# One step of a two-layer diffusion backbone: a new order of weights and of sums over k, and attention scores in double PSUM banks

## The chip, the core and the metric

The kernel runs on one core of a Trainium2 chip, with the engines TensorE (PE in the profile; its weight loads PEld), VectorE (DVE), ScalarE (ACT), GpSimd (POOL) and SyncE (SP, which issues the large loads). The metric is the device time of one execution in microseconds (us), the median of several; lower is better.

## What is computed

One step of a two-layer diffusion backbone on 640 tokens: 128 context tokens and 512 latent tokens, width 1024, all in fp32. The first 128 columns of every tile are context, the rest latent. Cut to what matters:

```python
for i in range(2):
    mod = (silu(cond) @ ada_w[i] + ada_b[i])        # 9 vectors of 1024, for c and for c_ctx
    h = rms_norm(x) * (1 + mod[1]) + mod[0]
    x = x + 0.5 * mod[2] * swiglu(h)                # ffn (i,0): 1024 -> 2 x 2816 -> 1024
    h = rms_norm(x) * (1 + mod[4]) + mod[3]
    x = x + mod[5] * (even_mixer(h) if i == 0 else odd_mixer(h))
    h = rms_norm(x) * (1 + mod[7]) + mod[6]
    x = x + 0.5 * mod[8] * swiglu(h)                # ffn (i,1)
# even mixer: 4 retention heads, and 4 groups of u * (w_s @ rms_norm(gelu(v)) + b_s)  ("SGU")
# odd mixer: 8 heads of differential attention over 640 keys:
s = einsum(q, k) * scale                            # two maps j = 0, 1 for each head
p = softmax(s);  a = p[0] - lam * p[1];  o = rms_norm(a @ v)
```

## The kernel before

**Products.** Activations lie with the features on the partitions and the 640 tokens in two halves of 320 columns. Every weight tile of 1 MB comes from HBM into one of two `raw` buffers, and is split in pieces of 128x1024 into a high part (`whi`, a copy on ACT, L308) and a low part (`wlo`, a subtraction on DVE, L309); five pieces may be live. Each product is then three matmuls (L695 high x high, L696 low x high, L697 high x low) of 128x320, accumulated in one PSUM bank.

**Stages.** ffn(0,0), even mixer, ffn(0,1), ffn(1,0), odd mixer, ffn(1,1). An ffn has 22 groups of 256 hidden features in chunks of 6, 8 and 8: for each group an input product ("fin", the last 19 groups by Strassen's scheme, evacuated to activations `a<l><s><g>h` and `...l`), and at the end of a chunk four output groups ("fout"), which sum over the chunk's groups. `out_proj` (L812) goes through the four, `op_step` (L837) through two column tiles j and two token halves hf of each: one PSUM tile `op...` for each (j, hf), all k of the chunk in a row, then the update of `xs` on DVE (L807).

**The order of weights.** One list, `order`, fixes it; SP loads a tile of it when a `raw` buffer is free (`pump`). Into the list `weave` (L223) puts the tiles of `ada_w` from which `mod` is made: one (`ads`) behind each entry that isn't a fin, and one (`pads`) ahead of each fin whose number stands in `FA`. A tile named in `ADV` is worked off on DVE (`ada_v`, L391: four passes over 128x1024, L404 for layer 0 and L406 for layer 1), others on PE (`ada`, L431: 32-column matmuls, L447, and at the fourth tile of a vector a copy to SBUF and two transposes). Each holds a `raw` buffer until it is done. In layer 1 vectors 0 to 5 are DVE's, 6 to 8 PE's.

**The engines' order.** Code is written in one thread with generators in the background (`spawn`, `tick`): each product of PE lets the background take a step. A scheduler sets the order on PE, DVE and ACT from that and from priorities (`high_priority(HP)`); SP's is the order in which it is written.

**Even mixer.** `sgu` (L1180) waits until its normalized `vs[g]` is ready, lets `SGW` = 11 steps pass and issues the mixing product `mx` (L1186). `load_condb` (L186) loads the conditioning, a tile of 128x2048, and runs Silu over it on ACT; it is called at the end of `first_wide`, the first product of ffn(0,0).

**Odd mixer.** A unit is one head and 128 queries: 8 heads of 4 full units (640 keys) and one of the context (128 keys). `sm_a` (L1292) takes for a full unit four PSUM tiles `as` of one bank of the eight (two maps j by two halves of the keys), runs 8 matmuls, four maxima on DVE (L1316), two minima (L1319) that join the halves, four exponentials on ACT with their sums (L1324); `sm_b` (L1328) joins the sums, and normalizes. Transposes, the product with the values and an rms norm of the head follow in the background, and the output groups ("oout", PSUM tiles `oo`) are woven between.

**Prologue.** `first_wide` and the code from L1500 on make the first two vectors of `mod` from PE, normalize x and begin ffn(0,0); two pieces there and two in `first_wide` are split with GpSimd as the subtracting engine (`split_piece(nc.gpsimd)`).

## Time and profile before

| | us |
|---|---|
| median of 3 runs | 2477.71 (2469.72 to 2481.81) |
| profiled execution, its time | 2478.16 |
| profiled execution, its span | 2476.1 |
| TensorE busy / weight load busy | 2395.3 (97%) / 2342.1 (95%) |
| VectorE busy | 1840.8 (74%) |
| ScalarE busy | 1067.4 (43%) |
| GpSimd busy | 63.7 (3%) |
| mean granted clock of TensorE | 0.987 |

The span runs from the first to the last instruction of the profiled execution; the time has some 2 us around it. A matmul's shown duration runs past the start of the next one, since they are pipelined; what a stretch of matmuls costs is read from their starts, and what a wait costs from the idle time ahead of the instruction that waited.

### The profile page before, as it was taken

The numbers are of one execution on the slowest core, as the hardware profiler recorded it, in microseconds if no ns is written. First come the engines' busy times: TensorE is split into PE (matmuls) and PEld (weight loads), VectorE is DVE, ScalarE is ACT, GpSimd is POOL, SyncE is SP. The second block draws the span as 40 slices with busy tenths as digits, with TensorE's granted clock in tenths as the row PEclk, the third lists the DMA queues.
The fourth block names the chain that finished last, engine by engine and source line by source line (L and its number), as shares of the span: only waits on it lengthen the run. The fifth ranks groups of instructions, "written<-read, shape, count | busy, mean of one in ns | idle before, by whom it ended". The sixth has DMA issues, their size and how long they took to land.

```text
span 2476.1 us, 40714 instructions
## 1 busy us (share of the span) xinstructions
PE 2395.3 (97%) x16530; PEld 2342.1 (95%) x16530; DVE 1840.8 (74%) x3749; ACT 1067.4 (43%) x2018; POOL 63.7 (3%) x86
## 2 busy tenths in 40 slices
PE   8999999999899999999999999999999999999998
PEld 6899999899899999999999999999999989999998
DVE  7677867877878777677977776789788878574664
ACT  4525335333226335153542423536777646252442
POOL 1000000000000000000000000001011000000000
PEclk8999999999999999999999999999999999999999
DMA  7342423323231433423234242242111111222121
GB/s 277 112 151 86 154 71 115 137 105 124 79 136 69 137 120 119 153 96 124 91 108 145 96 175 89 103 171 74 42 43 57 54 35 67 81 87 91 69 103 43
DMA packets 44476, 259.30 MB, mean 105 GB/s; under 512 B 5889, under 2 KB 8577, under 8 KB 16769
## 3 DMA queue, kind: packets, MB, share of 16 engines
q1 hardware_dynamic: 41024, 252.37, 28.6%
q8 instruction: 129, 2.11, 0.4%
q0 software_dynamic: 1280, 2.62, 0.3%
q10 hardware_dynamic: 1984, 1.72, 0.2%
q14 instruction: 59, 0.48, 0.1%
HBM read 252.76 MB, written 3.93 MB: 104 GB/s over the span
## 4 chain that ended last, share of the span: by engine, by line
PE 80%; DVE 9%; DMA 4%; ACT 4%; issue 2%; POOL 0%; POOLq 0%; ACTq 0%; DVEq 0%
PE op L696 8%; PE op L697 8%; PE op L695 8%; PE pu L695 6%; PE pu L696 6%; PE pu L697 6%; PE pg L697 3%; DVE wlo L309 3%; PE pg L696 3%; PE pg L695 3%; PE pf L695 3%; PE pf L696 3%; PE pf L697 3%; ACT whi L308 2%; DMA raw<-in_w_fout 2%
## 5 line engine op out<-in xcount | busy, mean ns | idle before, releaser
L309 DVE TENSOR_TENSOR wlo<-raw,whi 128x1024 fp32r<-128x1024 f32 (+1 forms) x480 | 528.8, 1118 | 286.0 <-ACT whi L308 284.9
L308 ACT ACTIVATE whi<-raw 128x1024 fp32r<-128x1024 f32 (+1 forms) x484 | 465.0, 976 | 639.7 <-DMA raw<-in_w_fout 144.1
L807 DVE SCALAR_TENSOR_TENSOR xs<-op,mod,xs 128x128 f32<-128x128 f32 (+2 forms) x312 | 126.9, 435 | 135.1 <-PE op L697 134.6
L524 ACT ACTIVATE nq<-xs 128x320 f32<-128x320 f32 x84 | 39.0, 468 | 135.1 <-DVE xs L807 133.3
L406 DVE CUSTOM_DVE_ANT_0 raw<-raw,sb 128x1024 f32<-128x1024 f32 x72 | 87.4, 1218 | 0.7
L404 DVE SCALAR_TENSOR_TENSOR raw<-raw,sb 128x1024 f32<-128x1024 f32 x72 | 87.5, 1220 | 0.5
L695 PE MATMUL oq<-H4h,whi 128*128 128x320 f32 x256 | 81.1, 318 | 0.2 <-ACT ov L979 0.2
L697 PE MATMUL oq<-H4h,wlo 128*128 128x320 f32 x256 | 79.6, 311 | 0.0
L696 PE MATMUL oq<-H4l,whi 128*128 128x320 f32 x256 | 79.3, 310 | 0.0
L1316 DVE TENSOR_REDUCE amx<-as 128x1 f32<-128x320 f32 x144 | 61.5, 460 | 19.1 <-PE as L1312 18.8
L1324 ACT ACTIVATE ap<-as,anm 128x320 f32<-128x320 f32 x128 | 66.2, 531 | 14.1 <-DVE anm L1319 13.9
L696 PE MATMUL pf<-H5p,whi 128*128 128x320 f32 x172 | 53.8, 313 | 2.0 <-DVE H5p L614 2.0
L871 ACT COPY p<-pg 128x320 f32<-128x320 f32 x76 | 32.5, 427 | 53.8 <-PE pg L697 53.6
L696 PE MATMUL pf<-H3p,whi 128*128 128x320 f32 x172 | 53.5, 312 | 1.8 <-DVE H3p L614 1.8
L696 PE MATMUL pf<-H2p,whi 128*128 128x320 f32 x172 | 53.4, 312 | 1.8 <-DVE H2p L614 1.8
L695 PE MATMUL pf<-H0p,whi 128*128 128x320 f32 x172 | 54.3, 318 | 0.2 <-ACT H0p L609 0.2
L696 PE MATMUL pf<-H0p,whi 128*128 128x320 f32 x172 | 53.9, 313 | 0.2 <-DVE H0p L614 0.2
L695 PE MATMUL pf<-H5p,whi 128*128 128x320 f32 x172 | 53.9, 317 | 0.0
L695 PE MATMUL pf<-H3p,whi 128*128 128x320 f32 x172 | 53.8, 317 | 0.0
L695 PE MATMUL pf<-H2p,whi 128*128 128x320 f32 x172 | 53.8, 316 | 0.0
L291 DVE TENSOR_TENSOR raw<-raw 128x512 f32<-128x512 f32 x76 | 52.4, 689 | 1.9
L697 PE MATMUL pf<-H0p,wlo 128*128 128x320 f32 x172 | 53.8, 313 | 0.0
(2691 smaller groups left out, 8835.6 us busy)
## 6 DMA issues: line engine op xcount, KB each, us to landing
raw<-in_w_fin SPq DMA_DIRECT2D x88, 1024.0 KB, 4.7
raw<-in_ada_w SPq DMA_DIRECT2D x64, 1024.0 KB, 4.8
raw<-in_w_fout SPq DMA_DIRECT2D x32, 1024.0 KB, 4.7
raw<-in_w_fout SPq DMA_DIRECT2D x16, 768.0 KB, 4.1
raw<-in_w_oin SPq DMA_DIRECT2D x12, 1024.0 KB, 4.8
...
```

Source lines behind the costliest of these rows:

```text
L291: sub.tensor_tensor(out=a11, in0=a22, in1=a11, op=ALU.subtract)
L308: S.activation(out=hf, in_=t, func=AF.Copy)
L309: sub.tensor_tensor(out=lf, in0=t, in1=hf.bitcast(F32), op=ALU.subtract)
L404: V.scalar_tensor_tensor(out=o, in0=w, scalar=1.0, in1=sb[:, c * D:(c + 1) * D], op0=ALU.mult, op1=ALU.mult, accum_out=r)
L406: V.tensor_tensor_reduce(out=o, in0=w, in1=sb[:, c * D:(c + 1) * D], scale=1.0, scalar=0.0, op0=ALU.mult, op1=ALU.add, accum_out=r)
L524: S.activation(out=q[:, :n], in_=x[k][:, t0:t1], func=AF.Square)
L695: PE.matmul(o, wh, xh, start=start, stop=False, skip_group_check=more)
L696: PE.matmul(o, wh, xl, start=False, stop=False, skip_group_check=more)
L697: PE.matmul(o, wl, xh, start=False, stop=stop, skip_group_check=more)
L807: V.scalar_tensor_tensor(out=x[m][:, a:b], in0=ps[:, a - t0:b - t0], scalar=mod[:, l, gmod * KD + m, c:c + 1], in1=x[m][:, a:b], op0=ALU.m ...
L1316: V.tensor_reduce(out=mx[:, j, a:a + 1], in_=sps[j][a][:, 0:w], axis=AX.X, op=ALU.max, negate=True)
L1324: S.activation(out=pj[j][:, a * 320:a * 320 + w], in_=sps[j][a][:, 0:w], func=AF.Exp, bias=b, accum_out=(sm[:, j, a:a + 1] if full else s2 ...
```

## The change

Seven edits:

1. **Order of the ada tiles.** `FA` gets eight places. Vector 2 of layer 1 leaves `ADV`, so its four tiles go to PE, and the tiles are dealt out anew: vectors 0, 1, 3, 4, 5 behind entries, 2, 6, 7, 8 ahead of fins. `weave` skips the entry ("fout", chunk 0, group 3) of ffn(0,1) and ffn(1,0), so that no ada tile lies between it and the next chunk's first fin; before, one for DVE lay there and one for PE ahead of fin 6.
2. **Scores.** PSUM pools are opened for a phase (`banks`): while heads are worked off, two tiles of two banks (`wide`) and four of one; otherwise eight of one. A unit's map j has its 640 scores in one `wide` tile, with one maximum over both banks and one exponential. Minima and sums that joined halves go.
3. **End of the odd mixer.** Before the pool changes back, `finish_all()` runs all that is left in the background; then the second half of the output groups begins.
4. **Prologue.** All subtractions are DVE's; one high part is made early (`split_hi`), and norm and split are put in another order, some with high priority.
5. **`load_condb`** is called after the input product of group 4 of ffn(0,0).
6. **`op_wide`.** For the first fout group of each chunk of n groups, all four (j, hf) sum k = 0 to n-3, then all four k = n-2, then a background ada step, then all four k = n-1 with the updates of `xs`.
7. **`SGW`** is 30.

The core of the diff:

```diff
-FA = (4, 6, 9, 12, 14, 18)
+FA = (4, 8, 10, 12, 15, 16, 18, 20)
-SGW = 11
+SGW = 30
-ADV = {(0, g) for g in range(12, 36)} | {(1, g) for g in range(24)}
+ADV = {(0, g) for g in range(12, 36)} | {(1, g) for g in range(24) if g // 4 != 2}
...
-            if ads and w[0] != "fin" and not (w[0] == "ein" and w[1] < 2):
+            if ads and w[0] != "fin" and not (w[0] == "ein" and w[1] < 2) and w[3:] not in skip:
...
-    l1, pl = ada_groups(1, range(6)), ada_groups(1, range(6, 9))
+    l1, pl = ada_groups(1, (0, 1, 3, 4, 5)), ada_groups(1, (2, 6, 7, 8))
...
-    order += weave(ffn_order(0, 1), l1[:12], pl[:6], FA)
-    order += weave(ffn_order(1, 0), l1[12:], pl[6:], FA)
+    order += weave(ffn_order(0, 1), l1[:11], pl[:8], FA, ((0, 3),))
+    order += weave(ffn_order(1, 0), l1[11:], pl[8:], FA, ((0, 3),))
...
+    def banks(wide_):
+        ps_.close()
+        pool["n"] = 8 - 4 * wide_
...
+    def wide(name):
+        return pool["p"].tile([P, 1024], F32, tag="w", bufs=2, name=name)
...
-                split_piece(nc.gpsimd)
-                split_piece(nc.gpsimd)
+                split_piece()
+                split_piece()
...
-        load_condb()
...
+            if gi == 0 and keys[0][0] == "fout":
+                op_wide(keys[0], W, acts, l, gmod, nxt)
+                continue
...
+    def op_wide(key, W, acts, l, gmod, nxt):
+        n = len(acts)
+        cuts = ((0, n - 2), (n - 2, n - 1), (n - 1, n))
+        jh = [(j, hf) for j in range(2) for hf in range(2)]
+        ps = {}
+        for c, (a, b) in enumerate(cuts):
+            for j, hf in jh:
+                if c == 0:
+                    ps[j, hf] = psm("op" + "_".join(str(v) for v in key[1:]) + f"_{j}{hf}")
+                for k in range(a, b):
+                    mm3(ps[j, hf], W, j, k, acts[k], hf, k == 0, k == n - 1)
+                if c == 2:
+                    op_end(ps[j, hf], j, hf, l, gmod, nxt)
+            if c == 1:
+                mid_ada()
+        W.done()
...
+                if i == 0 and g == 4:
+                    load_condb()
...
-            sps = [[psm(f"as{nm}{j}{a}") for a in range(ni)] for j in range(2)]
+            sps = [wide(f"as{nm}{j}") for j in range(2)]
...
-                for a in range(ni):
-                    V.tensor_reduce(out=mx[:, j, a:a + 1], in_=sps[j][a][:, 0:w], axis=AX.X, op=ALU.max, negate=True)
...
+                sv = sps[j].rearrange("p (a c) -> p a c", a=2)[:, 0:ni, 0:w]
+                V.tensor_reduce(out=nmx[:, j:j + 1], in_=sv, axis=AX.XY, op=ALU.max, negate=True)
+                yield
+                S.activation(out=pj[j][:, :ni * w].rearrange("p (a c) -> p a c", a=ni), in_=sv, func=AF.Exp,
+                             bias=nmx[:, j:j + 1], accum_out=s2[:, j:j + 1])
...
         finish(p0)
+        banks(1)
...
+        finish_all()
+        banks(0)
         Ws = [next_group(("oout", 1, 0))]
```

**How instructions move: PE, ffn(0,0), first output group of chunk 0.** `op0_0_0_0_<j><hf>` are its PSUM tiles, `a000h` to `a005l` the high and low activations of the six groups. Before, from the fourth activation of the first tile on:

```order
L695 MATMUL op0_0_0_0_00_1344<-a003h_935,whi18_1_1284 128x320
L696 MATMUL op0_0_0_0_00_1344<-a003l_936,whi18_1_1284 128x320
L697 MATMUL op0_0_0_0_00_1344<-a003h_935,wlo18_1_1285 128x320
L695 MATMUL op0_0_0_0_00_1344<-a004h_1078,whi18_1_1284 128x320
L696 MATMUL op0_0_0_0_00_1344<-a004l_1079,whi18_1_1284 128x320
L697 MATMUL op0_0_0_0_00_1344<-a004h_1078,wlo18_1_1285 128x320
L695 MATMUL op0_0_0_0_00_1344<-a005h_1213,whi18_1_1284 128x320
L696 MATMUL op0_0_0_0_00_1344<-a005l_1214,whi18_1_1284 128x320
L697 MATMUL op0_0_0_0_00_1344<-a005h_1213,wlo18_1_1285 128x320
L695 MATMUL op0_0_0_0_01_1376<-a000h_341,whi18_0_1232 128x320
```

and now, at the same place:

```order
L720 MATMUL op0_0_0_0_00_1344<-a003h_933,whi18_1_1284 128x320
L721 MATMUL op0_0_0_0_00_1344<-a003l_934,whi18_1_1284 128x320
L722 MATMUL op0_0_0_0_00_1344<-a003h_933,wlo18_1_1285 128x320
L720 MATMUL op0_0_0_0_01_1361<-a000h_341,whi18_0_1232 128x320
L721 MATMUL op0_0_0_0_01_1361<-a000l_342,whi18_0_1232 128x320
L722 MATMUL op0_0_0_0_01_1361<-a000h_341,wlo18_0_1233 128x320
L720 MATMUL op0_0_0_0_01_1361<-a001h_344,whi18_0_1232 128x320
L721 MATMUL op0_0_0_0_01_1361<-a001l_345,whi18_0_1232 128x320
L722 MATMUL op0_0_0_0_01_1361<-a001h_344,wlo18_0_1233 128x320
L720 MATMUL op0_0_0_0_01_1361<-a002h_797,whi18_0_1232 128x320
```

The last two activations of the first tile (`a004`, `a005`) have moved behind the first four activations of all four tiles, which is 3 x 4 x 4 = 48 matmuls ahead of the first one on `a004`; with eight groups in a chunk it is 72.

**DVE, ffn(0,0), first output group of chunk 2.** `xs` rows with `op0_0_2_0_..` are that group's updates; `adaj0_20` and `raw51` are the four passes of an ada tile that holds a load buffer; rows without either are the even mixer's tables. Before:

```order
L807 SCALAR_TENSOR_TENSOR xs_74<-op0_0_2_0_00_4235,mod_92,xs_74 128x320
L404 SCALAR_TENSOR_TENSOR adaj0_20_4285,mod_92<-raw51_4107,sb_91 128x1024
L1026 TENSOR_SCALAR dn_4254<-dq_4251 128x12
L404 SCALAR_TENSOR_TENSOR raw51_4107,mod_92<-raw51_4107,sb_91 128x1024
L1027 TENSOR_TENSOR dn_4254<-dn_4254,dq_4251 128x12
L404 SCALAR_TENSOR_TENSOR raw51_4107,mod_92<-raw51_4107,sb_91 128x1024
L807 SCALAR_TENSOR_TENSOR xs_74<-op0_0_2_0_01_4287,mod_92,xs_74 128x192
L807 SCALAR_TENSOR_TENSOR xs_74<-op0_0_2_0_01_4287,mod_92,xs_74 128x128
L1043 TENSOR_SCALAR dq_4251<-dq_4251 128x12
L1031 TENSOR_SCALAR ds2_4306<-dz_4253 128x12
L404 SCALAR_TENSOR_TENSOR raw51_4107,mod_92<-raw51_4107,sb_91 128x1024
L1032 RECIPROCAL ds2_4306<-ds2_4306 128x12
```

and now:

```order
L831 SCALAR_TENSOR_TENSOR xs_74<-op0_0_2_0_01_4276,mod_92,xs_74 128x128
L1094 SCALAR_TENSOR_TENSOR lg_4353<-dacc_4308,dq_4251 128x12
L831 SCALAR_TENSOR_TENSOR xs_74<-op0_0_2_0_10_4298,mod_92,xs_74 128x320
L831 SCALAR_TENSOR_TENSOR xs_74<-op0_0_2_0_11_4337,mod_92,xs_74 128x192
L831 SCALAR_TENSOR_TENSOR xs_74<-op0_0_2_0_11_4337,mod_92,xs_74 128x128
L1100 TENSOR_TENSOR dta0_4356<-dta0_4356,rc0_4247 128x256
L1101 TENSOR_TENSOR DT_4355<-dta0_4356 128x128
L429 SCALAR_TENSOR_TENSOR adaj0_20_4397,mod_92<-raw51_4107,sb_91 128x1024
L1100 TENSOR_TENSOR dta1_4367<-dta1_4367,rc0_4247 128x256
L1100 TENSOR_TENSOR dta2_4378<-dta2_4378,rc0_4247 128x256
L429 SCALAR_TENSOR_TENSOR raw51_4107,mod_92<-raw51_4107,sb_91 128x1024
L831 SCALAR_TENSOR_TENSOR xs_74<-op0_0_2_1_00_4437,mod_92,xs_74 128x320
```

The ada tile's passes began behind the first update; now they begin behind all updates of the group, and the next group's updates lie among them.

**PE, end of the odd mixer.** `oo071` ends the first half of the output groups, `oo1..` are the second half, `oo4h` to `oo6h` the heads 4 to 6, `aot7a` and `aot7b` transposes of head 7. Before:

```order
L697 MATMUL oo110_20890<-oo6h_20852,wlo202_1_20580 128x320
L695 MATMUL oo111_20894<-oo6h_20852,whi202_1_20579 128x320
L696 MATMUL oo111_20894<-oo6l_20853,whi202_1_20579 128x320
L697 MATMUL oo111_20894<-oo6h_20852,wlo202_1_20580 128x320
L987 MATMUL aot7a_20953<-cst_79,aon7_20619 128x128 x4
L987 MATMUL aot7b_20954<-cst_79,aon7_20619 128x128
L695 MATMUL oo140_20993<-oo4h_19942,whi203_0_20879 128x320
L696 MATMUL oo140_20993<-oo4l_19943,whi203_0_20879 128x320
L697 MATMUL oo140_20993<-oo4h_19942,wlo203_0_20880 128x320
```

and now:

```order
L720 MATMUL oo071_20512<-oo3h_19672,whi201_1_19862 128x320
L721 MATMUL oo071_20512<-oo3l_19673,whi201_1_19862 128x320
L722 MATMUL oo071_20512<-oo3h_19672,wlo201_1_19863 128x320
L1036 MATMUL aot7a_20554<-cst_79,aon7_20292 128x128 x4
L1036 MATMUL aot7b_20555<-cst_79,aon7_20292 128x128
L720 MATMUL oo100_20571<-oo4h_19689,whi202_0_20201 128x320
L721 MATMUL oo100_20571<-oo4l_19690,whi202_0_20201 128x320
L722 MATMUL oo100_20571<-oo4h_19689,wlo202_0_20202 128x320
L720 MATMUL oo101_20579<-oo4h_19689,whi202_0_20201 128x320
```

Before, 36 matmuls on heads 4 to 6 (`oo100` to `oo111`) stood between the last `oo071` and head 7's transposes; now the transposes follow `oo071` at once, and the 36 stand behind.

In the whole program PE gets 32 ada matmuls and two transposes more. DVE loses the passes of four ada tiles (16), 64 maxima, 64 minima and 32 sums, and gets four subtractions that were GpSimd's; ACT loses 64 exponentials. The product `mx` of the SGU's first group moves 93 instructions of PE later.

## Rows read from the trace of the kernel before

**Rows 1.** The page: busy time of the engines, and the chain that ended last by engine (shares of the span).

```profile
PE 2395.3 (97%) x16530; PEld 2342.1 (95%) x16530; DVE 1840.8 (74%) x3749; ACT 1067.4 (43%) x2018; POOL 63.7 (3%) x86
PE 80%; DVE 9%; DMA 4%; ACT 4%; issue 2%; POOL 0%; POOLq 0%; ACTq 0%; DVEq 0%
```

**Rows 2.** Windows, the whole odd mixer (columns: the stretch, its length, PE, PEld, DVE, ACT, POOL busy with the number of instructions, PE's granted clock, share of the DMA engines, GB/s).

```profile
1660.00:2005.00 345.00, 337.96 (x2442) 325.72 (x2441) 288.81 (x792) 228.40 (x646) 41.17 (x58) 1.00 0.16 56
```

**Rows 3.** Waits of PE over the whole run: what waited, for whom, us in total, times, the longest. Of the nine rows of 1.0 to 1.1 us with `op` and an activation `a...` of this list, the first and the last; then the first and the last of the four of 0.2 to 0.5.

```profile
PE mx L1186 <- DVE evs L1005: 7.5, 1, 7.5
PE adaps L460 <- DVE adac L457: 5.8, 2, 4.5
PE pg L695 <- ACT whi L308: 5.4, 2, 2.8
PE n50p L543 <- DVE nq L528: 2.9, 1, 2.9
PE adaps L447 <- ACT a000s L905: 2.8, 1, 2.8
PE op L695 <- ACT whi L308: 2.5, 2, 2.0
...
PE op L696 <- DVE a1021l L891: 1.1, 1, 1.1
...
PE op L695 <- ACT a005h L890: 1.0, 1, 1.0
...
PE op L696 <- DVE a105l L891: 0.5, 1, 0.5
...
PE op L696 <- DVE a115l L891: 0.2, 1, 0.2
```

**Rows 4.** The same view, of 130 to 1660 us only.

```profile
PE pg L697 <- DVE wlo L309: 1.4, 2, 0.7
```

**Rows 5.** Windows behind three waits: that of `mx`, the first of `pg` (and the stretch after it), and that of `n50p` (columns as in rows 2).

```profile
631.70:635.10 3.40, 2.90 (x13) 2.93 (x14) 2.94 (x16) 0.00 (x0) 0.00 (x0) 0.50 0.64 263
887.70:891.10 3.40, 3.40 (x14) 3.40 (x14) 1.23 (x1) 1.19 (x2) 0.00 (x0) 0.50 0.70 226
891.10:895.00 3.90, 3.90 (x28) 3.90 (x28) 2.81 (x5) 1.42 (x3) 0.00 (x0) 1.00 0.17 71
2007.20:2010.60 3.40, 3.40 (x14) 3.40 (x15) 2.28 (x20) 0.00 (x0) 0.00 (x0) 0.51 0.85 289
2010.60:2014.10 3.50, 3.50 (x15) 3.50 (x15) 1.67 (x6) 0.47 (x1) 0.00 (x0) 0.51 0.05 19
```

**Rows 6.** Timeline of SP's loads around the end of chunk 0 of ffn(0,1): the loads from fin 6 on (start, length to the last of them, queue, line, operation, tile and count).

```profile
873.58 14.40 SPq L267 DMA_DIRECT2D raw<-in_w_fin  x3
```

**Rows 7.** Timeline of DVE and then of ACT at that place: the fourth pass over the ada tile, and the first high part of fin 6 (in brackets the idle time before, and who ended it).

```profile
872.32 1.22 DVE L406 CUSTOM_DVE_ANT_0 raw<-raw,sb 128x1024 f32<-128x1024 f32 x1
878.40 1.58 ACT L308 ACTIVATE whi<-raw 128x1024 fp32r<-128x1024 f32 x2 [17.93 <-DMA raw<-in_w_fin]
```

**Rows 8.** Window that ends with the wait of `mx` in the even mixer (columns as in rows 2).

```profile
600.00:633.00 33.00, 25.53 (x183) 25.36 (x182) 31.58 (x97) 5.85 (x11) 0.00 (x0) 0.93 0.33 117
```

**Rows 9.** Timelines of POOL and DVE in the prologue, 44 to 51 us.

```profile
44.33 4.95 POOL L309 TENSOR_TENSOR wlo<-raw,whi 128x1024 fp32r<-128x1024 f32 x2 [17.85 <-ACT whi L308]
47.18 2.44 DVE L586 TENSOR_TENSOR H0t<-H0t,H0t 128x320 f32<-128x320 f32 x1
49.66 0.49 DVE L587 TENSOR_TENSOR H0t<-H0t,H0t 128x320 f32<-128x320 f32 x1
```

**Rows 10.** Timeline of ACT at the end of `first_wide`, and the ada matmuls of PE that stand there, of the window from 64 to 90 us (minimum, median and maximum of one in ns, first and last start).

```profile
71.15 1.89 ACT L188 ACTIVATE sb<-sb 128x2048 f32<-128x2048 f32 x1
L447 PE MATMUL adaps<-raw,sc x32: 379/379/403, 73.4 to 75.0; 128*32 128x256 f32 x32
```

**Rows 11.** Groups of instructions by line in the odd mixer (1660 to 2005 us): busy us, mean ns of one, idle time before them and what ended it.

```profile
L1324 ACT ACTIVATE ap<-as,anm 128x320 f32<-128x320 f32 x128 | 66.2, 531 | 14.1 <-DVE anm L1319 13.9
...
L1312 PE MATMUL as<-ok,oq 128*128 128x320 f32 x128 | 41.0, 340 | 3.2 <-ACT ap L1324 2.8 <-ACT aaT L1355 0.5
...
L1324 ACT ACTIVATION_READ_ACCUMULATOR ap<-as,anm 128x1 f32 x128 | 26.5, 207 | 0.0
...
L1316 DVE TENSOR_REDUCE amx<-as 128x1 f32<-128x320 f32 x128 | 57.2, 482 | 15.2 <-PE as L1312 14.8
```

**Rows 12.** Timelines of PE, ACT and DVE at the end of the odd mixer: the first of the 36 matmuls on heads 4 to 6 and the transposes behind them; head 7's squares, their sums, and its normalized blocks.

```profile
1984.99 0.31 PE L695 MATMUL oo<-oo4h,whi 128*128 128x320 f32 x1
...
1990.43 1.12 PE L987 MATMUL aot7a<-cst,aon 128*128 128x128 f32 x4
1984.75 0.72 ACT L992 ACTIVATE ao7q<-aon 128x640 f32<-128x640 f32 x1
1986.21 0.81 DVE L995 TENSOR_REDUCE ao7m<-ao7q 128x5 f32<-128x640 f32 x1
...
1990.03 1.40 DVE L1007 SCALAR_TENSOR_TENSOR aon<-aon,ao7r,subln_sb 128x128 f32<-128x128 f32 x5
```

**Rows 13.** Timelines of DVE and SP in chunk 2 of ffn(0,0): the fourth pass over its first ada tile, and two of the loads that follow.

```profile
439.76 1.22 DVE L404 SCALAR_TENSOR_TENSOR raw<-raw,sb 128x1024 f32<-128x1024 f32 x1
441.02 0.33 SPq L267 DMA_DIRECT2D raw<-in_w_fout  x1
...
462.43 0.33 SPq L267 DMA_DIRECT2D raw<-in_w_fout  x1
```

More of the change, by code (lines that the diff above doesn't have):

```diff
@@ L107, in trunk_kernel @@
     tp = ctx.enter_context(tc.tile_pool(name="tp", bufs=1))
-    pp = ctx.enter_context(tc.tile_pool(name="pp", bufs=1, space=PSUM))
     ctx.enter_context(tc.manual_schedule(engines={mybir.EngineType.SP}))
@@ L129, in tiny @@
         return tp.tile(shape, dt, tag="y" if n <= 8 else "yy", bufs=35 if n <= 8 else 8, name=name)
+    ps_ = ctx.enter_context(ExitStack())
+    pool = {}
+    def banks(wide_):
+        ps_.close()
+        pool["n"] = 8 - 4 * wide_
+        pool["p"] = ps_.enter_context(tc.tile_pool(name=f"pp{wide_}{len(pool)}", bufs=1, space=PSUM))
+        pool[len(pool)] = 0
+    banks(0)
+    def wide(name):
+        return pool["p"].tile([P, 1024], F32, tag="w", bufs=2, name=name)
     def psm(name):
-        return pp.tile([P, 512], F32, tag="b", bufs=8, name=name)
+        return pool["p"].tile([P, 512], F32, tag="b", bufs=pool["n"], name=name)
     bgs = []
@@ L221, in ffn_order, with weave @@
         return r
-    def weave(ws, ads, pads=(), fins=()):
+    def weave(ws, ads, pads=(), fins=(), skip=()):
         r, ads, pads = [], list(ads), list(pads)
@@ L272, in pump, with skip_raw, split_hi, split_piece @@
             emit_load()
-    def split_piece(sub=V):
+    def skip_raw():
         while st["sp"] < nord and order[st["sp"]][0] == "ada":
             st["sp"] += 1
+    pre = {}
+    def split_hi(j, h):
+        hi = pre[j, h] = wp.tile([P, 1024], F32R, tag="whi", bufs=5, name=f"whi{j}_{h}")
+        t = raw[j].rearrange("p (m h x) -> p h m x", m=2, h=2)[:, h]
+        S.activation(out=hi.rearrange("p (m x) -> p m x", m=2), in_=t, func=AF.Copy)
+    def split_piece(sub=V):
+        skip_raw()
         j = st["sp"]
@@ L301, in split_piece @@
             t = r[:, h * n:(h + 1) * n]
-        hi = wp.tile([P, 1024], F32R, tag="whi", bufs=5, name=f"whi{j}_{h}")
+        early = pre.pop((j, h), None)
+        hi = early or wp.tile([P, 1024], F32R, tag="whi", bufs=5, name=f"whi{j}_{h}")
         lo = wp.tile([P, 1024], F32R, tag="wlo", bufs=5, name=f"wlo{j}_{h}")
@@ L307, in split_piece @@
             hf, lf = hi[:, :n], lo[:, :n]
-        S.activation(out=hf, in_=t, func=AF.Copy)
+        if early is None:
+            S.activation(out=hf, in_=t, func=AF.Copy)
         sub.tensor_tensor(out=lf, in0=t, in1=hf.bitcast(F32), op=ALU.subtract)
@@ L839, in op_step, with op_end @@
         mm_fm(ps, W, j, acts, hf, ks)
+        op_end(ps, 2 * gi + j, hf, l, gmod, nxt)
+    def op_end(ps, m, hf, l, gmod, nxt):
         if nxt is None:
[L841 removed]
+            x_update(ps, m, l, gmod, hf)
         else:
             with tc.high_priority(HP):
[L844 to L845 removed]
+                x_update(ps, m, l, gmod, hf)
+                norm_acc(nxt, hf, m)
     def strassen_in(i, l, s, g, e):
@@ L1311, in sm_a @@
                         k = kh[2 * q + j][:, a * 320:(a + 1) * 320] if full else kp[rows, c * P:(c + 1) * P]
-                        PE.matmul(sps[j][a][:, 0:w], qh[j][rows, qs], k, start=(q == 0), stop=(q == 1))
+                        PE.matmul(sps[j][:, a * 512:a * 512 + w], qh[j][rows, qs], k, start=(q == 0), stop=(q == 1))
             yield
             for j in range(2):
-                for a in range(ni):
-                    V.tensor_reduce(out=mx[:, j, a:a + 1], in_=sps[j][a][:, 0:w], axis=AX.X, op=ALU.max, negate=True)
-                    yield
-                if full:
-                    V.tensor_tensor(out=nmx[:, j:j + 1], in0=mx[:, j, 0:1], in1=mx[:, j, 1:2], op=ALU.min)
-                    b = nmx[:, j:j + 1]
-                else:
-                    b = mx[:, j, 0:1]
-                for a in range(ni):
-                    S.activation(out=pj[j][:, a * 320:a * 320 + w], in_=sps[j][a][:, 0:w], func=AF.Exp, bias=b,
-                                 accum_out=(sm[:, j, a:a + 1] if full else s2[:, j:j + 1]))
+                sv = sps[j].rearrange("p (a c) -> p a c", a=2)[:, 0:ni, 0:w]
[3 more added lines that the diff above has]
+                             bias=nmx[:, j:j + 1], accum_out=s2[:, j:j + 1])
                 yield
@@ L1329, in sm_b @@
             hd, qb = u
-            pj, sm, s2 = sres[u]
+            pj, s2 = sres[u]
             nk = T if qb < 4 else P
             nm = f"{hd}{qb}"
-            if qb < 4:
-                V.tensor_tensor(out=s2, in0=sm[:, :, 0], in1=sm[:, :, 1], op=ALU.add)
             rs = tiny([P, 2], "ars" + nm)
@@ L1524, in trunk_kernel @@
         pass
-    split_piece(nc.gpsimd)
-    split_piece(nc.gpsimd)
+    skip_raw()
+    split_hi(st["sp"], 0)
     warm(WU[2])
@@ L1537, in trunk_kernel @@
         t = stmp(f"bcs{hf}")
-        S.copy(out=t[:, :t1 - t0], in_=bc[:, :t1 - t0])
+        with tc.high_priority(HP):
+            S.copy(out=t[:, :t1 - t0], in_=bc[:, :t1 - t0])
         bcs[0, hf] = t
@@ L1550, in apply_all2 @@
                 q()
-    apply_all2((0, 1))
+    with tc.high_priority(HP):
+        norm_apply(0, 0, 0)()
+        split_piece()
+        norm_apply(0, 1, 0)()
+    apply_all2((1,))
+    split_piece()
     tb[0] = spawn(tbuild(0))
```

8 lines of the change are left out of this document (2 added, 6 removed).

## The prediction

> **What bounds the kernel.** First the page: PE is busy for 97% of the span, and 80% of the chain that ended last is PE's, against 9% of DVE and 4% each of ACT and DMA [rows 1]. So time is worth something only where PE stands still, or where its clock is low. Second the waits of PE: the largest are one of 7.5 us for `mx`, two for the first product `pg` of a chunk (5.4 for the high part, 1.4 for the low one), thirteen at the first output group of a chunk, and a few singles [rows 3, 4]. Third the windows behind such waits: 28 matmuls pass in 3.9 us at the full clock, 2.4 GHz, but 14 in 3.4 us where 0.50 was granted, 1.2 GHz, right after PE had stood still [rows 5]. 14 matmuls are worth 14/28 x 3.9 = 1.95 us, so such a stretch loses 1.45 us. A long wait costs itself and this. The change removes some of these waits and puts new ones in other places. I sum against the profiled execution, 2478.16, which is 0.45 above the median.
>
> **Output groups (`op_wide`).** Nine waits of 1.0 to 1.1 us and four of 0.2 to 0.5 are for the activation of the last group of a chunk, which PE reaches at once [rows 3]; added up from that view, 9.4 + 1.5 = 10.9 us. At the end of the odd mixer 36 matmuls take 1990.43 - 1984.99 = 5.44 us [rows 12], 0.151 us each; the 48 that now go first (chunk of six) are 7.2 us, the 72 (chunk of eight) 10.9. Either hides 1.1 us, and most of it is still hidden if DVE falls back by 5 us. **-10.9**.
>
> What the new order gives back: in chunk 2 of ffn(0,0) the fourth pass over the ada tile ended at 440.98, and SP's next load went out at 441.02, since only then a buffer was free [rows 13]. The new order puts these passes behind all updates of the group, which come in its last eighth. A group of eight is 96 matmuls, 14.5 us; four passes of 1.22 us behind it, with updates between, end 20 to 24 us into the chunk, not 7. From load to high part a tile took 878.40 - 873.58 = 4.8 us [rows 6, 7], and the split takes one to two more: 26 to 31 us, where PE wants it after two groups, at 29. So PE waits 0 to 2 us, and 1.45 of low clock may follow. The wait for the last group's weights, which is there already (the 2.0 in the row of 2.5 us [rows 3]), moves with its load of 462.43 [rows 13], up or down. I take **+3**, between 0 and +6. In other chunks the passes stay early in DVE's order.
>
> **No ada tile at the chunk change.** The load of fin 6 went out at 873.58, when the fourth pass of an ada tile (872.32, 1.22 us) had freed its buffer, and its high part began at 878.40 [rows 6, 7]; PE waited for weights 2.6 and 0.7 us. With nothing between, fin 6 follows fout 3 into the ring. Two such places: 5.4 + 1.4, and a low stretch of 1.45 behind each (measured for the first, taken for the second): **-9.7**. The ada tiles that left stand elsewhere; two are now neighbours, ahead of fins 15 and 16. PE works these off itself within a microsecond, so a buffer comes free at once; I cost it at nothing, and 2 us if its load comes late.
>
> **Four ada tiles from DVE to PE.** 32 records of the ada matmul run from 73.4 to 75.0 [rows 10], 1.65 us; a tile is 16 records, so four are 64, 3.3 us, and for two transposes I add 0.2 (four of head 7's stand at 1.12 with their run-out [rows 12]): **+3.5**, all on PE. DVE loses 16 passes of 1.22 us, 19.5 us; it isn't the limit there, and I give nothing for it.
>
> **SGU.** `mx` waits 7.5 us, and the 13 matmuls behind it run at 0.50: 2.9 us of work that is worth 1.8 [rows 3, 5]; together 8.6. The 93 instructions that now go first can fill it, but part of them are retention products that wait for DVE too, which was busy for 31.58 of the 33 us ahead [rows 8]. Between 0 and 4 us stay; I take 1.2: **-7.4**.
>
> **Prologue.** While POOL subtracts (44.33, 4.95 us for two), one 320-column operation of DVE takes 2.44 us, where the next of the same size takes 0.49 [rows 9]; behind them stands the wait of 4.5 us for `adac` [rows 3]. DVE gets the subtractions itself, some 1.2 us each. I take 1 us of gain. Silu over the conditioning holds ACT for 1.89 us [rows 10] just ahead of the evacuation for which PE waits 2.8 [rows 3]: gone there, -1.7; at group 4 it may hold up another evacuation, up to 3 us. Together **-2.7**, from -5 to +1.
>
> **Scores.** A unit had four maxima of 0.48 and four exponentials of 0.53 with a readout of 0.21 [rows 11]. The nearest rows for 640 columns are 0.81 (a sum on DVE) and 0.72 (squares on ACT) [rows 12], so DVE and ACT each save half a microsecond or so in each of 32 units. Neither is the limit: in 345 us DVE is busy for 289, ACT for 228, PE for 338 [rows 2]. What PE can get back is its wait for a score bank, 3.2 us [rows 11]. Against it: two `wide` tiles are one unit's. The next unit's first score has to wait until maximum and exponential have read the tile: 0.8 + 0.75 + 0.2 and the hand-overs, some 2 us behind the last score. In the new order of PE nine of 39 changes of unit have less than that of other work between them (by matmuls at 0.15 us); they lack 7.5 us in all. 7.5 - 3.2, less some 3 that I allow, with no row to show it, for 64 tiles that PE no longer takes over one by one: **+1**, from -6 to +8.
>
> Here a page speaks against the change. The wait for a score bank is small, 3.2 us, and repeats [rows 11]. The Trainium skill, "Perfetto Trace Analysis", section "Optimization Strategy", says that the same gap coming back on the engine that should be full can mean that PSUM doesn't suffice for the next tile; by that, two double tiles in place of single ones make it worse, and the sum would be that of the second rival below. The same page, section "Optimizing Scalar/DVE Operations", says that larger operations help where their engine is saturated, and that where ACT or DVE merely cause bubbles elsewhere, smaller ones may finish sooner: here neither is full [rows 2]. I hold with the rows, since most changes of unit have other work between them.
>
> **End of the odd mixer.** 36 matmuls covered head 7's norm, whose blocks came at 1990.03 [rows 12]; now PE reaches the transposes 5.4 us earlier with nothing in between. It waits 3.5 to 5.3 us (less if DVE's other work moves away), and 1.45 to 2.9 us of low clock follow. Against it: behind the mixer `n50p` waits 2.9 us for DVE [rows 3], and 29 matmuls take 6.9 us at 0.51, which are worth 4.0 [rows 5]; 5.8 us, of which most should go, as DVE empties its queue during the new wait. I take 7.3 - 5.8: **+1.5**, from -1 to +8.
>
> **Sum.** -10.9 + 3 - 9.7 + 3.5 - 7.4 - 2.7 + 1 + 1.5 = -21.7 us: 2456.5, and 2456.0 against the median. I round to **2455**; single waits under 0.2 us aren't in the sum.
>
> **Rivals.** *The waits move.* SGU keeps 4 us (+2.8), chunk 2 pays its 6 (+3), the end of the mixer pays 8 (+6.5): 2467. For it: DVE is as good as full ahead of `mx`. Against it: the cover in the new orders is several times the waits. *The scores wait at every unit.* Each of the 39 changes exposes the chain of 2 us by half or more: +1 us each, 39 us, 2494, slower. It decides from 21.7/39 = 0.56 us on that the gain is gone. For it: one unit fills both tiles. Against it: in 30 of 39 places the order has 2 us and more of other matmuls, and the heads' work is spread. *Better than costed.* Scores at -6, the prologue at -5: 2446. *It doesn't do what it says.* The activation comes later by as much as PE, since DVE is the one behind; then `op_wide` gives nothing, 2466. Against it: DVE is busy for 74% [rows 1], and 1 us is all that PE waits.
>
> **How the numbers follow.** Forecast (2447 to 2462) 0.60; better 0.14; moved waits (2462 to 2472) 0.15; no gain from `op_wide` 0.05; scores at every unit 0.06. A measurement tells about 0.5% from no change here, 12.4 us: faster is under 2465.3, which holds the first two and half of the third, 0.81; same 0.14; slower 0.05. The range, 2442 to 2467, leaves out the scores' case, half of the moved waits' upper part and the low end.
>
> **What would show it.** PE's waits without the thirteen for `a...` at `op`, without `pg` for `whi` and with `mx` at 0 to 4; `adaps` for `a000s` at 1 or less; a new wait for `aot7a` of 3.5 to 5.3 and `n50p` gone; `as` for `ap` at 5 to 10 in few places; `op0_0_2_2` for `whi` at 0 to 2. Wrong if waits for `ap` are found at most unit changes, if low clock follows waits that I counted as small, or if `n50p` stays.

## The result, and the profile after

The changed kernel took 2459.26 us (median of 7, 2456.8 to 2468.84), the kernel before 2479.16 beside it (7 runs). The ratio is 0.9932, with a 95% interval of 0.9917 to 0.9946: faster, by more than half a per cent. The profiled execution took 2456.8 us, its span is 2455.0; against the profiled one of before that is 21.4 us less, where -21.7 had been summed up. It is the fastest of its seven, though: by the medians it is 19.9 us, and the readings by stage below are of this one execution.

The page of the changed kernel, busy time and chain [rows 1]:

```profile
PE 2388.3 (97%) x16596; PEld 2337.1 (95%) x16596; DVE 1809.7 (74%) x3563; ACT 1050.4 (43%) x1890; POOL 56.3 (2%) x82
PE 85%; DVE 7%; ACT 3%; DMA 2%; issue 2%; POOL 0%; POOLq 0%; ACTq 0%; SPq 0%; DVEq 0%
```

More of the chain is PE's, and less DVE's and DMA's. The waits of PE over the whole run (columns as in [rows 3]):

```profile
PE adaps L472 <- DMA raw<-in_ada_w: 6.4, 2, 5.0
PE aot7a L1036 <- DVE aon L1056: 5.3, 1, 5.3
...
PE n20p L568 <- DVE nq L553: 3.5, 1, 3.5
PE op L720 <- ACT whi L333: 3.2, 1, 3.2
...
PE as L1359 <- ACT ap L1365: 2.5, 7, 0.9
PE oq L720 <- ACT okr L1003: 2.4, 1, 2.4
...
PE pf L721 <- DVE H2p L639: 1.8, 1, 1.8
...
PE pg L720 <- ACT whi L333: 1.5, 1, 1.5
PE n50b L580 <- DVE n50d L577: 1.4, 1, 1.4
PE adaps L472 <- ACT a000s L952: 1.4, 1, 1.4
...
PE oo L720 <- ACT aof L1446: 0.5, 1, 0.5
```

Read it against [rows 3]: `mx` isn't there any more, nor is any `op` that waits for an activation `a...`; `pg` for `whi` has lost both its places (the 1.5 is a new one, in ffn(0,0)). Of the rows that are new or have grown, three bear on the argument most: `aot7a` for `aon`, `oq` for `okr`, and `op` for `whi` with 3.2 in one. The largest row of all, `adaps` for its load, stands in the first 26 us; before, it was 4.5, which [rows 3] passes over.

By stage, from the start of the first product of each: ffn(0,0) with the prologue is 2.1 us shorter (494.6 to 492.5 at the even mixer's first product), the even mixer 9.7, ffn(0,1) 6.1, ffn(1,0) 8.4, ffn(1,1) 3.2. The odd mixer is 8.4 us **longer**. Its three parts are the products ahead of the first score, the attention, and from the first output group to ffn(1,1); first before, then after (columns as in [rows 2]):

```profile
1664.90:1725.00 60.10, 59.15 (x424) 58.35 (x423) 55.32 (x132) 35.31 (x76) 9.11 (x13) 1.00 0.21 74
1725.00:1926.50 201.50, 196.89 (x1446) 188.57 (x1445) 165.90 (x459) 141.78 (x425) 28.74 (x41) 1.00 0.15 50
1926.50:2022.10 95.60, 92.00 (x625) 88.79 (x625) 75.96 (x238) 53.52 (x150) 3.32 (x4) 0.96 0.14 46
```

```profile
1638.60:1702.80 64.20, 60.88 (x425) 59.92 (x424) 56.90 (x132) 37.03 (x81) 12.23 (x15) 0.97 0.20 69
1702.80:1904.30 201.50, 194.78 (x1450) 188.86 (x1449) 155.81 (x336) 128.93 (x322) 27.30 (x39) 1.00 0.15 50
1904.30:2004.20 99.90, 90.96 (x622) 88.07 (x621) 74.59 (x198) 50.29 (x119) 3.80 (x4) 0.95 0.13 44
```

The middle part is where the edit that the title names does most of its work: 216 of the 288 score matmuls stood in it before, 220 do now (the rest are in the third part). DVE is busy 10 us less and ACT 13 us less, and the part is as long as before to a tenth of a microsecond. The loss is at the two ends, 4.1 and 4.3 us, where the pools change.

### The profile page after: what moved, and what is told of

It is laid out like the page before. It is cut to its first block, busy times and chain, and to the rows that moved or that the text cites. A ratio compares the mean times of both kernels' runs of the same rounds, so it can differ in the third digit from the quotient of the medians.

```text
span 2455.0 us, 40549 instructions
## 1 busy us (share of the span) xinstructions
PE 2388.3 (97%) x16596; PEld 2337.1 (95%) x16596; DVE 1809.7 (74%) x3563; ACT 1050.4 (43%) x1890; POOL 56.3 (2%) x82
## 4 chain that ended last, share of the span: by engine, by line
PE 85%; DVE 7%; ACT 3%; DMA 2%; issue 2%; POOL 0%; POOLq 0%; ACTq 0%; SPq 0%; DVEq 0%
PE op L720 8%; PE op L721 8%; PE op L722 8%; PE pu L720 7%; PE pu L721 7%; PE pu L722 7%; PE pg L722 3%; PE pg L721 3%; PE pg L720 3%; PE pf L721 3%; PE pf L720 3%; PE pf L722 3%; DVE wlo L334 2%; DMA raw<-in_w_fin 1%; PE oq L720 1%
## 5 line engine op out<-in xcount | busy, mean ns | idle before, releaser
L333 ACT ACTIVATE whi<-raw 128x1024 fp32r<-128x1024 f32 (+2 forms) x483 | 462.3, 975 | 607.4 <-PE op L721 143.5
L1363 DVE TENSOR_REDUCE anm<-as 128x1 f32<-128x640 f32 (+1 forms) x80 | 56.8, 712 | 35.9 <-PE as L1359 35.2
L431 DVE CUSTOM_DVE_ANT_0 raw<-raw,sb 128x1024 f32<-128x1024 f32 x60 | 72.9, 1219 | 0.7
L1365 ACT ACTIVATE ap<-as,anm 128x640 f32<-128x640 f32 (+1 forms) x80 | 57.1, 715 | 11.8 <-DVE anm L1363 11.3
L721 PE MATMUL pf<-H5p,whi 128*128 128x320 f32 x172 | 53.2, 310 | 1.8 <-DVE H5p L639 1.8
L721 PE MATMUL pf<-H2p,whi 128*128 128x320 f32 x172 | 52.9, 310 | 1.8 <-DVE H2p L639 1.8
L314 DVE TENSOR_TENSOR raw<-raw 128x512 f32<-128x512 f32 x76 | 52.3, 688 | 1.5
L312 DVE TENSOR_TENSOR raw<-raw 128x512 f32<-128x512 f32 x76 | 52.2, 687 | 1.4
L722 PE MATMUL pf<-H5p,wlo 128*128 128x320 f32 x172 | 53.1, 309 | 0.0
```

Of the source, the lines that this page charges most:

```text
L312: sub.tensor_tensor(out=a22, in0=a21, in1=a22, op=ALU.add)
L314: sub.tensor_tensor(out=a11, in0=a22, in1=a11, op=ALU.subtract)
L333: S.activation(out=hf, in_=t, func=AF.Copy)
L431: V.tensor_tensor_reduce(out=o, in0=w, in1=sb[:, c * D:(c + 1) * D], scale=1.0, scalar=0.0, op0=ALU.mult, op1=ALU.add, accum_out=r)
L721: PE.matmul(o, wh, xl, start=False, stop=False, skip_group_check=more)
L722: PE.matmul(o, wl, xh, start=False, stop=stop, skip_group_check=more)
```

## The experiments

Differences below are of medians, beside 2459.26 for the changed kernel, where not said otherwise; the kernel before was 2477.3 to 2478.6 beside them, and 2479.16 beside the changed one, so such a difference is uncertain by 2 us from this alone. Where the interval of a ratio overlaps that of the changed kernel (0.9917 to 0.9946), the time shows no difference for certain, and the argument rests on the waits.

**Scores and pools as before.** Edits 2 and 3 are undone, the rest stays.

```diff
-            sps = [wide(f"as{nm}{j}") for j in range(2)]
+            sps = [[psm(f"as{nm}{j}{a}") for a in range(ni)] for j in range(2)]
...
-        banks(1)
...
-        finish_all()
-        banks(0)
```

> The changed kernel with edits 2 and 3 undone: four single banks per unit, eight single banks throughout, nothing run out at the end of the mixer. Theory: these two edits cost the odd mixer 8.4 us (1664.9 to 2022.1 before is 357.2 us, 1638.6 to 2004.2 after is 365.6), 4 at its start for want of single banks (wait of 2.39 us for okr at 1672, with low clock) and the rest at its end (5.29 us for aot7a): the time is 2459 - 8 = 2451 us, ratio to before 0.989, and aot7a, and oq for okr, don't wait. Rival: DVE and ACT are freed by the wide instructions, and the stage is longer for another reason (the tiles of ada that moved, the weights): 2459 or more, and the stage stays near 365.

Measured: 2449.77 us (2447.67 to 2451.73), ratio 0.9885 [0.9871, 0.99]. The windows of the same three parts of this run:

```profile
1639.60:1699.60 60.00, 59.06 (x423) 58.26 (x423) 54.20 (x130) 35.24 (x75) 9.09 (x13) 1.00 0.22 74
1699.60:1901.00 201.40, 196.82 (x1445) 188.50 (x1444) 165.79 (x459) 141.70 (x425) 28.67 (x41) 1.00 0.15 50
1901.00:1996.60 95.60, 92.00 (x626) 88.78 (x625) 76.10 (x238) 53.60 (x150) 3.31 (x4) 0.96 0.14 47
```

The three parts are those of before again, 357.0 us. The theory holds: edits 2 and 3 cost 8 to 9 us, none of it in the middle part. This kernel beats both. (Double banks without a change of pools were not run.)

**Pool changed later.** Is the wait of `oq` a shortage of single banks? The pool is opened only ahead of the first unit.

```diff
-        finish(p0)
-        banks(1)
+        finish(p0)
...
             if at is None:
                 finish(p1)
+                banks(1)
```

> The changed kernel, but the pool of four single and two double banks is opened just before the first unit of attention, behind the products of the first three heads' queries and keys. Theory (single banks run short there): the wait of 2.39 us of oq for okr at 1672 goes, and with it a low stretch: 4 us less, 2455. Rival: okr is late because ACT is busy with weights, whatever the banks: the wait and 2459 stay.

Measured: 2466.74 us (2461.64 to 2472.68), ratio 0.995 [0.9932, 0.9968]. PE's waits from 1638 to 1710 us:

```profile
PE ov0p L823 <- ACT okr L1003: 5.7, 1, 5.7
```

Both fell: the wait neither went nor stayed. It went along with the call, to the first tile behind it (`ov0p`), and grew to 5.7. That gave a new theory, which the next run tells from the shortage.

**The same pool closed and opened.** In the kernel with the scores as before, the pool of eight single banks is closed and opened again where the changed kernel changes it.

```diff
         finish(p0)
+        banks(0)
```

> The run of the changed kernel with scores as before (2449.8), and one thing more: where the changed kernel changes its pool at the start of the mixer, the pool of eight single banks is closed and opened again, the same as it was. New theory (closing a pool is a barrier: the first tile of the next one waits until what was written last in the old one has been read): a wait of oq for okr of 2 to 3 us near 1672, with low clock behind it: +4 us, 2454. Old theory (four single banks are too few there): no such wait, 2450.

Measured: 2459.04 us (2456.26 to 2462.61), ratio 0.9934 [0.9908, 0.996]. The waits of the same stretch:

```profile
PE oq L720 <- ACT okr L1003: 2.4, 1, 2.4
```

```profile
1641.80:1704.40 62.60, 59.27 (x424) 58.29 (x423) 55.44 (x130) 35.38 (x78) 11.00 (x14) 1.00 0.21 71
```

All eight banks are there, and the wait of the changed kernel stands at its place with its length. So it is the closing of a pool that costs: the next tile waits for the last reader of the old pool. What it costs is 2.6 us here (62.6 against 60.0), where the clock stays at 1.00, and 4.1 in the changed kernel, where low clock follows the same wait. The two profiled executions are 5.9 us apart: the mixer's first two parts show 3.6 of it (the second is 202.4 against 201.4), the third is 95.6 in both, and 2.2 lie ahead of the mixer, where the kernels have the same instructions. The medians are 9.3 us apart; the pool is not shown to cost that much.

**Run out at the end, without a pool.** In the same kernel, `finish_all()` alone.

```diff
+        finish_all()
         Ws = [next_group(("oout", 1, 0))]
```

> The run of the changed kernel with scores as before (2449.8), and finish_all() ahead of the second half of the output groups, without any change of pool; head 7's transposes then stand right behind oo071 again. Theory (the order costs it): a wait of about 5 us for aot7a, with low clock behind; n50p, 2.92 in that run, falls to under 1.5: +3 to +5 us, 2453 to 2455. Rival (the wait is the pool's): no wait for aot7a over 1.5 us, 2450.

Measured: 2454.41 us (2453.25 to 2459.76), ratio 0.9916 [0.9894, 0.9938]. PE's waits from 1900 to 2010 us:

```profile
PE aot7a L1036 <- DVE aon L1056: 5.3, 1, 5.3
```

```profile
1904.00:2001.10 97.10, 89.77 (x626) 86.77 (x625) 76.88 (x238) 53.89 (x151) 3.31 (x4) 0.98 0.13 46
```

The theory holds for the wait: it has its full length without any change of pool, so it comes from the order of PE, in which head 7's transposes stand ahead of the 36 matmuls. The size is less certain. The medians are 4.6 us apart, but the intervals of the two ratios overlap, and the third part of the mixer is 97.1 us against 95.6. In the changed kernel it is 99.9, with more low clock (0.95), and the pool adds a wait of its own there: `oo` for `aof`, 0.5 us, which this run hasn't.

**Partial sums in the double tiles.** The 36 matmuls go ahead of the transposes again, in the double tiles, and the pool is changed behind them.

```diff
-        finish_all()
-        banks(0)
+        ow = [wide(f"oo1w{n}") for n in range(2)]
...
-                        pss[gi, j] = psm(f"oo1{gi}{j}")
+                        pss[gi, j] = ow[gi][:, 512 * j:512 * j + 512]
...
+                elif gp == 0:
+                    finish_all()
+                    banks(0)
```

> The changed kernel, but the four partial sums of the second half of the output groups lie in the two double tiles, so that their matmuls can stand ahead of head 7's transposes; the background is run out and the pool changed only after the first of these groups. Some of the 36 matmuls then stand even earlier; 24 stand between head 6's transposes and head 7's, 3.5 us. Theory: the wait of 5.29 us for aot7a falls to 1 to 2.5 us and its low clock may go: 3 to 6 us less, 2453 to 2456. Rival (what is gained there is lost again at the norm behind the mixer, as n50p had waited 2.9 us before): 2458 to 2461, with a longer wait of n50p or n50b.

Measured: 2461.0 us (2458.85 to 2464.44), ratio 0.9936 [0.9919, 0.9952]. PE's waits from 1900 to 2010 us:

```profile
PE aot7a L1036 <- DVE aon L1056: 2.9, 1, 2.9
PE n50b L580 <- DVE n50d L577: 1.4, 1, 1.4
PE oo1w L720 <- ACT oo7h L533: 1.3, 1, 1.3
...
PE oo L720 <- DVE xs L831: 0.6, 1, 0.6
```

The wait fell by 2.4 us, where 2.8 to 4.3 were forecast, and other waits took its place: the sums on head 7 wait for its high part (1.3), and the first tile of the new pool for the last update (0.6). From the first output group to ffn(1,1) it is 100.5 us, against 99.9 in the changed kernel. The rival's time is right, though the loss isn't at the norm, as it had it: `n50b` is what it was.

**Chunk 2 as before.** A single execution.

```diff
-            if gi == 0 and keys[0][0] == "fout":
+            if gi == 0 and keys[0][0] == "fout" and keys[0][1:4] != (0, 0, 2):
```

> The changed kernel, but chunk 2 of ffn(0,0) sums its first output group as before. One look for the waits. Theory (the ada tile's passes stand behind the updates, so a load goes out late): the passes end near 7 us into the chunk again, SP's next load goes out then and not 25.5 us in, and the wait of 3.17 us for the second group's weights goes; 1.1 for the last activation and up to 2 for the fourth group's weights come back. Rival (the loads are late for another reason, ahead of the chunk): the wait for the second group's weights stays at about 3.

Measured: 2458.28 us, one run. SP's load behind the passes, in the changed kernel and here:

```profile
451.83 0.33 SPq L280 DMA_DIRECT2D raw<-in_w_fout  x1
```

```profile
437.68 0.33 SPq L280 DMA_DIRECT2D raw<-in_w_fout  x1
```

And PE's waits from 420 to 500 us here:

```profile
PE op L720 <- ACT whi L333: 1.8, 1, 1.8
PE op L721 <- DVE a0021l L938: 1.1, 1, 1.1
```

The theory holds. With the passes early the load goes out 14 us sooner, and the 3.2 us at the third group (457.8 us) become 1.8 at the fourth (465.0) and 1.1 at the start. (The expectation calls the third group the second.) From the chunk's first output matmul to the even mixer's first product it is 64.3 us here, 66.2 in the changed kernel, 64.8 before: what `op_wide` gained there was lost. (The 7 us of the expectation, and of the prediction, is a misreading: the passes end 11.2 us into the chunk, 440.98 - 429.8 before and as much here.)

**Cover and early passes together.** The kernel with scores as before, and `op_wide` in this chunk by column tiles.

```diff
+        for part in (jh[:2], jh[2:]) if key[1:4] == (0, 0, 2) else (jh,):
...
+                if c == 1 and part[0] == (0, 0):
+                    mid_ada()
```

> The run of the changed kernel with scores as before (2449.8), and in chunk 2 of ffn(0,0) alone op_wide goes by column tiles: the two halves of j = 0 first (36 matmuls of cover, 5.3 us), then those of j = 1. In DVE's order the ada tile's passes then stand around the first update again. Theory (late passes, late load): the waits of 3.2 and 0.7 us for the second group's weights go, and their low clock; at the fourth group 0 to 2.5 come back: 2445 to 2449. Rival (the wait only moves to the fourth group with its whole price): 2450.

Measured: 2451.34 us (2448.6 to 2460.26), ratio 0.9897 [0.9881, 0.9914]: no better than without it. PE's waits from 420 to 500 us:

```profile
PE n10p L568 <- DVE nq L553: 2.3, 1, 2.3
PE op L720 <- ACT whi L333: 1.7, 1, 1.7
PE op L722 <- DVE wlo L334: 0.9, 2, 0.7
```

The rival's time is right. Again a wait was taken away (1.1 and 3.2 us), and the next ones in the row showed: what came back at the fourth group (1.7 + 0.9) is about what the theory allowed, but the norm behind it now waits 2.3, which neither had.

**Without `op_wide`.**

```diff
-            if gi == 0 and keys[0][0] == "fout":
-                op_wide(keys[0], W, acts, l, gmod, nxt)
-                continue
```

> The changed kernel without edit 6: every output group sums k in a row, as before. Theory (the last activation is late, and other k hide it): thirteen waits of 0.2 to 1.1 us, 10.9 in all, come back, the wait of 3.17 us for the second group's weights in chunk 2 of ffn(0,0) goes, one of some 2.5 for the fourth group's comes back: +8 to +10 us, 2468. Rival (once the other waits are gone, DVE is the one that is behind, and op_wide gains little): 2459 to 2462, and the waits reappear elsewhere.

Measured: 2474.88 us (2470.07 to 2483.56), ratio 0.9993 [0.9977, 1.001]. It costs 15.6 us, more than forecast. Some of PE's waits from 100 to 2300 us, and windows at the first output group of ffn(0,1), which begins at 828.8 us:

```profile
PE op L720 <- ACT a105h L934: 1.1, 1, 1.1
...
PE op L721 <- DVE a1113l L935: 1.0, 1, 1.0
```

```profile
832.00:835.40 3.40, 2.74 (x11) 2.51 (x12) 3.20 (x5) 0.17 (x1) 0.00 (x0) 0.71 0.81 301
835.40:838.80 3.40, 3.40 (x20) 3.40 (x20) 3.40 (x9) 0.00 (x0) 0.00 (x0) 0.78 0.02 5
```

The waits are back, thirteen of 0.4 us and more with 11.8 us, and two of 0.2. But here two of them, 1.1 and 0.4 us close together, are followed by a stretch of low clock, and so are the two at the first chunk of ffn(1,0) (0.51 from 1294.2 us on); in the profile of before, the same ones at the same places were not. That a wait of 1 us can cost 1.5 us more was in no term. This profile is of the slowest of the run's ten executions (2483.56 us), so it shows that such a price exists, and not how often it is paid.

**SGW = 11.**

```diff
-SGW = 30
+SGW = 11
```

> The changed kernel with SGW = 11, edit 7 undone. Theory (mx stood too early on PE): the wait of mx for evs comes back with about 7.5 us, and 1.1 of low clock: 2468. Rival (DVE is ahead by then, since other edits took work from it): the wait is under 4 us, 2463 or less.

Measured: 2469.48 us (2464.32 to 2477.32), ratio 0.9975 [0.9961, 0.9988]: 10.2 us, and the row of before word for word but for the line numbers:

```profile
PE mx L1235 <- DVE evs L1054: 7.5, 1, 7.5
```

The even mixer is 252.8 us long, 7.0 more than in the changed kernel. The theory holds; DVE is not ahead.

**Ada tiles as before.** Edit 1 undone.

```diff
-FA = (4, 8, 10, 12, 15, 16, 18, 20)
+FA = (4, 6, 9, 12, 14, 18)
...
-    order += weave(ffn_order(0, 1), l1[:11], pl[:8], FA, ((0, 3),))
+    order += weave(ffn_order(0, 1), l1[:12], pl[:6], FA)
```

> The changed kernel with edit 1 undone: ada tiles as before, vector 2 of layer 1 on DVE. Theory (an ada tile ahead of fin 6 made its load late): the two waits of pg for whi, 2.6 and 2.8 us with 0.7 each for wlo, and their low clock come back, 9.7 us, and four ada tiles of 1.1 us leave PE: +5 us, 2464. Rival (with the last activation hidden, PE comes to fin 6 earlier and waits longer still, or the load is early enough as DVE is ahead): over 2470, or 2459 and less.

Measured: 2464.02 us (2462.22 to 2466.95), ratio 0.9944 [0.9931, 0.9958]: 4.8 us. PE's waits from 800 to 1500 us:

```profile
PE pg L720 <- ACT whi L333: 3.7, 2, 2.2
PE pu L720 <- ACT whi L333: 2.9, 2, 1.5
...
PE pg L722 <- DVE wlo L334: 1.4, 2, 0.7
PE pu L722 <- DVE wlo L334: 1.4, 2, 0.7
```

The theory holds for the waits, and the time agrees, though the intervals overlap. The waits are 9.4 us where they had been 6.8: PE gets there earlier, as the first rival said, and waits at two products instead of one.

**Prologue and conditioning as before.** Edits 4 and 5 undone.

```diff
-                split_piece()
-                split_piece()
+                split_piece(nc.gpsimd)
+                split_piece(nc.gpsimd)
...
+        load_condb()
```

> The changed kernel with edits 4 and 5 undone: GpSimd subtracts the first four low parts, and the conditioning is loaded at the end of the first product. Theory (POOL slowed DVE, and Silu held ACT up): the first output group begins 2.9 us later, as before (130.8 against 127.9), 2462. Rival (the gain is used up by the waits of 1.1, 1.1 and 2.2 us that PE has behind it at 116, 122 and 174, since DVE isn't faster there): these waits shrink, and 2459 stays.

Measured: 2464.83 us (2460.95 to 2466.13), ratio 0.9943 [0.9928, 0.9958]: 5.6 us. PE's waits from 0 to 180 us:

```profile
PE adaps L485 <- DVE adac L482: 5.8, 2, 4.5
PE adaps L472 <- ACT a000s L953: 2.8, 1, 2.8
```

The two waits of before are back (3.8 and 1.4 in the changed kernel). The length of the second is no measure, though: in the run with scores as before, which has edits 4 and 5, it is 2.6 us too.

```profile
PE adaps L472 <- ACT a000s L952: 2.6, 1, 2.6
```

What the edits move is its end: 71.9 us here, 69.1 in the changed kernel, 68.5 in that run. The first output group begins at 129.8, 1.9 us later than in the changed kernel; so edits 4 and 5 are a gain of some 2 us. The 5.6 us between the medians can't be placed, and the intervals overlap.

## Why the prediction was right, and where it was not

**Output groups: right, mis-sized.** -10.9 forecast; taking it back costs 15.6. The waits are those of the sum, 11.8 and 10.9; for the rest the one profile shows two stretches of low clock behind waits of 1 us, where the sum gave low clock only to waits over 2. That they make up the difference in the medians is not shown.

**Chunk 2 of ffn(0,0): right.** Late passes, late load, wait. The load went out 25.5 us into the chunk, where the passes were to end at 20 to 24: more of DVE's other work lies between them. So the 3.2 + 0.4 us at the third group are above the 0 to 2 (and low clock) of the working; the stretch of 66.2 us against 64.8 before is +1.4, where -1.1 + 3 = +1.9 was forecast.

**Ada order: right.** -9.7 + 3.5 = -6.2; taking it back costs 4.8 in medians and 6.8 in spans (2461.8 - 2455.0). An ada tile takes 1.24 us between its neighbours' starts (1036.15 to 1037.39), 1.1 more than none, so the four are 4.4 and not 3.5:

```profile
1036.15 0.31 PE L722 MATMUL pu<-T23bh,wlo 128*128 128x320 f32 x1
1036.39 1.07 PE L472 MATMUL adaps<-raw,sc 128*32 128x256 f32 x16
1037.39 0.41 PE L720 MATMUL pu<-H2p,whi 128*128 128x320 f32 x1
```

The rows at 73.4 [rows 10], 32 in a row without a matmul of another kind between, were the wrong ones to take.

**SGU: right.** -7.4 with 1.2 kept; nothing is left of the wait. Of the 9.7 us by which the even mixer is shorter, 7.0 come back with `SGW` = 11. The doubt about DVE was not needed: 93 instructions on PE were enough for it.

**Prologue: right.** -2.7; the first output group begins 2.9 us earlier (127.9, 130.8 before), and 1.9 earlier than with edits 4 and 5 undone.

**Scores: the step that failed.** +1 was forecast, as a balance of waits at the units. The attention itself is at 0, as good as forecast: PE waits 2.5 us for exponentials in seven places, where 2.8 in five had been (the prediction took the whole 3.2 of [rows 11], of which 0.5 was for `aaT`). The 7.5 us that it had lacking at the changes of unit didn't appear; no run shows the 3 us that it allowed against them. Missing was the change of pool: 4.1 us (64.2 against 60.1) for a wait of 2.39 us with low clock behind it, 2.6 where the clock stayed. The prediction had looked at what the four single and two double banks hold, and not at the moment at which one set replaces the other. Of the two rules of the Trainium skill's page "Perfetto Trace Analysis" that were weighed, the one in "Optimization Strategy" (a repeated gap can mean too little PSUM) would have made the waits at the units worse, and they are not (2.5 us). The one in "Optimizing Scalar/DVE Operations" (larger operations help a saturated engine) agrees: DVE and ACT were freed, neither was saturated, and the time of the stage is the same.

**End of the mixer: right in its mechanism, mis-sized.** +1.5 forecast; +4.3 measured. The wait for `aot7a` is 5.3, the upper end; low clock behind it is longer than forecast, and of `n50p`'s 2.9 us 1.4 stay as `n50b`. The windows behind the wait, which ends at 1968.3 (the 3.8 us behind them have 0.85):

```profile
1968.40:1971.80 3.40, 2.88 (x10) 2.27 (x11) 1.54 (x5) 1.49 (x3) 0.00 (x0) 0.50 0.00 0
1971.80:1975.20 3.40, 3.40 (x14) 3.40 (x14) 0.12 (x1) 0.00 (x0) 0.00 (x0) 0.50 0.02 5
```

So the sum came out at the right place, with the odd mixer 6 us too cheap (8.4 against 2.5) and the gains elsewhere 5 us too small (29.5 by the stages against 24.2). That the two nearly cancel is luck, and most of the 5 us can't be put down to the edits. At the start of ffn(0,1), ffn(1,0) and ffn(1,1), `pf` waits 1.78 us for DVE (`H2p`, `H3p`, `H5p`), in both kernels alike. In the profile of before, a stretch of low clock follows each of the three waits; in that of the changed kernel none does. For the first of them, before and after:

```profile
768.20:771.60 3.40, 3.40 (x15) 3.40 (x15) 3.40 (x12) 3.40 (x9) 0.00 (x0) 0.50 0.00 0
```

```profile
756.40:759.80 3.40, 3.40 (x25) 3.40 (x24) 3.40 (x12) 3.40 (x9) 0.00 (x0) 1.00 0.00 0
```

In the same 3.4 us 15 matmuls pass in the one and 25 in the other; ten of 0.15 us are 1.5 us, and three times that is 4.5. In the thirteen profiles of this case 23 of these 39 waits are followed by low clock; with scores as before all three are, with `SGW` = 11 none.

Of the signs that the prediction named, four came out otherwise: `adaps` waits 1.4 for `a000s` and not 1 or less, `as` 2.5 for `ap` and not 5 to 10, the third group 3.2 for `whi` and not 0 to 2, and in place of `n50p` there is `n50b`.

Left open: single edits taken back add up to more than the whole. Scores and pools cost 9.5, the other edits that were taken back 15.6 + 10.2 + 4.8 + 5.6 = 36.2, which would leave 26.7, and 19.9 was measured. A wait that goes uncovers the next, so that an edit can be worth more when the others are there; and medians of four to ten executions spread by several us. These runs don't part the two.
